# Attention weights times values as three rounded products, and row sums turned through DRAM, in a hybrid mLSTM and attention encoder layer

## The chip, the cores and the metric

The kernel runs on one core of a Trainium2 chip. The metric is the device time of one execution in microseconds. Where three runs are shown, the median is given with the lowest and the highest. A profile is one execution taken by the hardware profiler; its span is the time between its first and last instruction.

The engines are named as in the profile: PE is TensorE (matmuls; PEld are its weight loads), DVE is VectorE, ACT is ScalarE, POOL is GpSimd, and SP is SyncE, which here only starts transfers. SPq, ACTq and POOLq are the instruction queues that start a DMA.

## The reference

One layer of an encoder is applied to 2048 prompt tokens and to 256 sample tokens with the same weights (D = 1024), and a final RMSNorm follows:

```
h = rmsnorm(x); p = h @ w_in
x = x + concat(mlstm(p), attention(p)) @ w_out          # 8 mLSTM heads, 8 attention heads of 64
h = rmsnorm(x); u = dwconv3(h @ w_up)                   # 2 x 2816 channels
x = x + (silu(g) * a) @ w_down ;  y = rmsnorm(x)
```

The change is in the attention. It has 8 query heads and 2 key/value heads, is bidirectional, and q and k are RMS-normed and rotated:

```
s = einsum('bqhgd,bkhd->bhgqk', q, k) * 64 ** -0.5      # per block of queries
p = softmax(s, axis=-1)
o = einsum('bhgqk,bkhd->bqhgd', p, v)
```

All inputs and outputs are float32. The prompt's 2048 queries see 2048 keys, the sample's 256 queries see 256 keys.

## The kernel before, in words

The 2304 tokens are 18 tiles of 128. A matmul of two float32 tiles is one product in the code and two matmul records in the profile. The large products are written as three *rounded* products instead (dtype float32r): an operand x is kept as hi = round(x) and lo = x - hi, and hi·hi + hi·lo + lo·hi are accumulated.

**Phase A** (`phase_a`, the first 230 us or so) takes one token tile after the other: `front_a` loads x and computes its mean square, `front_b` normalises it and splits it into hi and lo, `mm` multiplies it with the attention and gate columns of w_in, and `post_a`, `post_b`, `post2` make q, k and v and store them to DRAM (`q_d`, `k_d`, `v_d`). `gates` prepares the mLSTM gates. `gate_math` follows.

**Attention and mLSTM** run side by side (`run_both` takes steps of both generators in a fixed ratio). A planner with a timeline simulation then sets the order on each engine, by priorities and by when it takes an instruction to be ready. Each engine works through its own order. Parts of mLSTM have a raised priority (`MPRI`), and once the output projection runs, so has the attention (`APRI`).

The attention works in 36 blocks of 512 columns: 32 large ones (one head, 512 prompt queries, 16 key tiles) and 4 small ones (two heads, the 256 sample queries, 2 key tiles), so 32 x 16 + 4 x 2 = 520 key tiles in all. The small blocks of the first head group come first, those of the second come last. For each block:

- `prep` transposes q. `maxstep` multiplies queries with keys (tile px) and DVE takes the row maximum (L546, L547); the next block's 16 max steps are done during the present block. `prep2` turns the negated maxima into an extra row of the query operand.
- `scores` takes key tiles in pairs (a step, kp): two rounded products (L569, L570) put scores minus maximum into a PSUM tile ps, and ACT writes the exp to a float32 tile pe in SBUF (L571).
- `values`, two pairs later (`PLAG` = 2), multiplies pe with the value tile vv (L581), which holds 64 columns of v and 64 columns of ones; so rows 64 to 127 of the result pv are 64 copies of the softmax sum.
- `fin1` copies both halves of pv to SBUF (o1, rs: L589, L590). `fin2` takes the reciprocal of the 64x512 sums on DVE (L594), multiplies on POOL (L595) and stores to `mix_d` (L598).

The PSUM tiles with the tag "sc" (ps, px, the transposed q, and the maxima) share a ring of `SCB` = 4 banks, given out in the order of the program; pv has one bank. mLSTM has one bank for projections and two for the rest. `load_kv` loads keys and values of a head group over POOL's queue.

**Phase C** (`phase_c`) is the output projection. It begins when mLSTM is done and takes 256 tokens at a time, as soon as their attention output is complete: it loads `mix_d` (L934), splits it (L935, L936) and multiplies (L949), then adds x, squares and norms (L954, L957, L966). It still runs when the attention is finished. **Phase D** (from about 1900 us on) is the feed-forward part with the final norm; the change doesn't touch it.

Two lines of the kernel on which the attention's timing hangs, the ring and the lag:

```
ps = pp.tile([P, 512], F32, tag="sc", ...)      # ring of SCB = 4 PSUM banks, shared with px, pq, pr
if kp >= PLAG: values(cur, *todo.pop(0))        # PLAG = 2 pairs behind the scores
```

## Time and profile before

| | before |
|---|---|
| median of 3 runs | 3498.3 us (3497.74 to 3503.58) |
| the profiled execution's own time | 3496.09 us |
| its span | 3494.4 us |
| mean granted TensorE clock | 0.991 |
| PE busy | 3401.6 us, 97% |
| DVE busy | 2346.9 us, 67% |
| ACT busy | 1680.2 us, 48% |
| POOL busy | 1101.4 us, 32% |
| HBM read, written | 315.55 MB, 82.72 MB |

Busy times are sums over an engine's instructions without those that only start transfers, and overlapping instructions are counted once. Matmuls are pipelined: a matmul's own duration is longer than the time after which the next one starts, and the ends are modelled. The "granted clock" is the share of full speed that TensorE was given. In a list of groups a line reads: source line, engine, operation, output<-inputs, shapes and count, then the busy time and the mean duration in ns of one, then the idle time of the engine just before them and what ended it. In a list of waits: who waited, for whom, us in total, how many times, the longest.

### The profile page before, as it was taken

What the parts mean: (1) busy time and instruction counts of PE and PEld (TensorE: products, weight loads), DVE (VectorE), ACT (ScalarE), POOL (GpSimd) and SP (SyncE); (2) the same over time, 40 slices, a digit from 0 to 9 for tenths busy, and PEclk for the clock granted to TensorE, in tenths of its full rate; (3) what the DMA queues carried; (4) which work ended last, traced back from release to release, by engine and by line L of the source; (5) the groups of instructions that cost most, each with busy time, mean ns of one, the idle gap of its engine ahead of it and who ended that gap; (6) DMA issues with size and microseconds to landing.
All of it is one profiled execution on the core that took longest, in us unless ns stands there. A gap on an engine that the chain in (4) does not pass through costs nothing. (4 is left out here: it accounts for less than half of the span.)

```text
span 3494.4 us, 53250 instructions
## 1 busy us (share of the span) xinstructions
PE 3401.6 (97%) x19538; PEld 3027.3 (87%) x19538; DVE 2346.9 (67%) x4008; ACT 1680.2 (48%) x3809; POOL 1101.4 (32%) x1298
## 2 busy tenths in 40 slices
PE   7999999999999999999999999999999999999998
PEld 6788777777777777767788999998999999999998
DVE  6874364546544555664445888878888878887777
ACT  4544354444444454453333544445544445555555
POOL 6752022213231321311125333225433224422222
PEclk9999999999999999999999999999999999999999
DMA  6764233233243434442247332213423213312221
GB/s 218 244 196 135 81 119 96 83 119 95 89 128 111 136 112 136 130 138 79 86 157 249 120 105 96 73 69 122 143 98 103 73 67 124 140 63 70 73 68 54
DMA packets 252629, 401.76 MB, mean 115 GB/s; under 512 B 27984, under 2 KB 152688, under 8 KB 252368
## 3 DMA queue, kind: packets, MB, share of 16 engines
q1 hardware_dynamic: 220272, 355.87, 30.5%
q0 software_dynamic: 10640, 31.86, 3.1%
q10 hardware_dynamic: 21456, 10.62, 1.0%
q8 instruction: 154, 2.52, 0.3%
q14 instruction: 107, 0.88, 0.1%
HBM read 315.55 MB, written 82.72 MB: 114 GB/s over the span
## 5 line engine op out<-in xcount | busy, mean ns | idle before, releaser
L1203 PE MATMUL pd<-act,wd 128*128 128x384 f32 (+1 forms) x3120 | 591.2, 335 | 17.0 <-DVE acc L1205 11.3
L1203 PEld LDWEIGHTS pd<-act,wd 128*128 128x128 f32 x3120 | 539.5, 188 | 24.0 <-DVE acc L1205 14.7
L581 PE MATMUL pv<-pe,vv 128*128 128x512 f32 x1040 | 514.5, 593 | 0.2
L547 DVE TENSOR_REDUCE mx<-px 128x1 f32<-128x512 f32 (+1 forms) x528 | 342.5, 673 | 194.2 <-PE px L546 192.5
L1065 PE MATMUL pa<-nt,wut 128*128 128x386 f32 (+2 forms) x2376 | 455.0, 339 | 1.5 <-ACT u L1081 1.5
L1065 PEld LDWEIGHTS pa<-nt,wut 128*128 128x128 f32 x2376 | 422.2, 190 | 1.8 <-ACT u L1081 1.8
L571 ACT ACTIVATE pe<-ps 128x512 f32<-128x512 f32 x520 | 292.5, 595 | 262.2 <-PE ps L570 258.6
L1159 DVE SCALAR_TENSOR_TENSOR y<-u,cw,y 128x768 f32<-128x768 f32 (+1 forms) x264 | 307.9, 1167 | 36.0 <-ACT y L1152 29.0
L1070 POOL TENSOR_TENSOR tw<-ru 128x512 f32<-128x512 f32 x66 | 96.4, 1461 | 744.5 <-DMA ru<-w_up 536.5
L1205 DVE TENSOR_TENSOR acc<-pd,acc 128x384 f32<-128x384 f32 (+1 forms) x544 | 281.4, 538 | 37.5 <-PE pd L1203 36.5
L1081 ACT ACTIVATE u<-pa 128x386 f32<-128x386 f32 (+2 forms) x264 | 128.8, 488 | 327.1 <-PE pa L1065 325.0
L581 PEld LDWEIGHTS pv<-pe,vv 128*128 128x128 f32 x1040 | 189.0, 189 | 82.5 <-issue 57.8
L569 PE MATMUL ps<-qq,kk 128*128 128x512 f32 x520 | 249.8, 483 | 0.1
L949 PE MATMUL po<-cmx,wo 128*128 128x256 f32 x1728 | 241.7, 290 | 1.6 <-DVE wo L106 1.6
L949 PEld LDWEIGHTS po<-cmx,wo 128*128 128x128 f32 x1728 | 220.8, 190 | 25.4 <-issue 17.8
L546 PE MATMUL px<-kk,qq 128*128 128x512 f32 (+1 forms) x528 | 224.4, 455 | 2.6 <-ACT pe L571 1.7
L688 PE MATMUL mj<-mn,wm 128*128 128x256 f32 x1296 | 212.2, 303 | 5.8 <-ACT og L702 4.5
L688 PEld LDWEIGHTS mj<-mn,wm 128*128 128x128 f32 x1296 | 180.7, 193 | 34.7 <-issue 20.6
L570 PE MATMUL ps<-qm,kl 65*128 65x512 f32 x520 | 207.4, 402 | 0.0
L698 PE MATMUL mv<-wm,mn 128*128 128x256 f32 x1296 | 206.3, 298 | 0.9 <-ACT qb L694 0.9
L698 PEld LDWEIGHTS mv<-wm,mn 128*128 128x128 f32 x1296 | 178.4, 192 | 22.3 <-issue 14.2
L232 PE MATMUL pj<-w_a,n1T 128*128 128x512 f32 (+1 forms) x864 | 178.9, 362 | 5.7 <-ACT n1T L188 4.5
(283 smaller groups left out, 6629.8 us busy)
## 6 DMA issues: line engine op xcount, KB each, us to landing
ru<-w_up SPq DMA_DIRECT2D x132, 512.0 KB, 3.2
mn<-n_d SPq DMA_DIRECT2D x216, 256.0 KB, 3.3
rd<-w_down SPq DMA_DIRECT2D x66, 512.0 KB, 3.3
n_d<-n1T SPq DMA_DIRECT2D x18, 1024.0 KB, 5.6
dm<-nm_d POOLq DMA_DIRECT2D x72, 256.0 KB, 3.6
mjn<-n_d SPq DMA_DIRECT2D x72, 256.0 KB, 3.0
mvn<-n_d SPq DMA_DIRECT2D x72, 256.0 KB, 3.2
q_d<-qz SPq DMA_DIRECT2D x18, 512.0 KB, 3.1
```

The costliest lines, as they stand in the source:

```text
L546: nc.tensor.matmul(ps[:, 0:w], s.qq[:, t * P:(t + 1) * P], s.kv[z0][0][:, 0:w], start=True, stop=True)
L547: nc.vector.tensor_reduce(s.mx[:, t, z0:z0 + 1], ps[:, 0:w], AX.X, ALU.max)
L569: nc.tensor.matmul(ps[:, 0:N], kk[:, kc:kc + P], s.qq[:, 0:N], start=True, stop=False)
L571: nc.scalar.activation(pe[:, z, 0:N], ps[:, 0:N], AF.Exp)
L581: nc.tensor.matmul(s.pv[:, 0:N], s.kv[kp // 2][2][:, kt % 4, :], pe[:, z, 0:N], start=(kt == 0), stop=(kt == s.nk - 1))
L688: nc.tensor.matmul(pj[:, o], s.w[c][:, a, o * P:(o + 1) * P], nT[c][:, :, h, :], start=(c + o + k == 0), stop=(c == NCC - 1 and k == 2 and ...
L698: nc.tensor.matmul(pv[:, o], nT[c][:, o, a, :], s.w[c][:, h, 256:512], start=(c + o + k == 0), stop=(c == NCC - 1 and k == 2 and o == 1))
L949: nc.tensor.matmul(po[:, o], wo[c][z // 2][:, a, n], mx[c][:, h, :], start=(c == 0 and k == 0), stop=(c == NCC - 1 and k == 2))
L1065: nc.tensor.matmul(p, w[:, aa, c, :], ops[k][:, c, bb, 0:n], start=c == 0 and i == 0 and not add, stop=c == NCC // 2 - 1 and i == 2, skip_ ...
L1159: nc.vector.scalar_tensor_tensor(y[:, s:e], u[:, s + k:e + k], cw[:, k, jj:jj + 1], y[:, s:e], ALU.mult, ALU.add)
L1203: nc.tensor.matmul(po, wds[j][c // 4][:, aa, c % 4 * P:(c % 4 + 1) * P], acts[j][:, bb, z0:z1], start=(j == 0 and k == 0), stop=(j == len( ...
L1205: nc.vector.tensor_tensor(accs[c][:, z0:z1], po, accs[c][:, z0:z1], ALU.add)
```

## The change

What it does:

- **Values.** The exp is written back into its PSUM tile. ACT then copies it, rounded, to a tile ph in SBUF (`PHB` = 6 buffers), and DVE subtracts ph from the PSUM tile to a rounded tile pl (`PLB` = 6). v is stored as hi and lo in phase A (one more subtract on DVE; two stores over SP's queue instead of one over ACT's), loaded as two tiles, with ones in the hi tile's and zeros in the lo tile's extra columns. `values` makes three rounded products, vh·ph, vl·ph and vh·pl, of each float32 one.
- **Sums.** `fin1` copies one row of sums, and ACT's queue stores it to DRAM (`rs_d`). SP's queue loads it back as 128x4. `fin2` (at step 1 of the next block) takes the reciprocal of the 128x4 tile on DVE, stores it and loads it broadcast to 64 rows, both over SP's queue. `fin3` (at step 4, or at the block's last step) multiplies on POOL and stores to `mix_d`.
- **Phase A.** x is loaded by `load_x`, one tile earlier, over SP's queue for the first four tiles and over POOL's from then on. Of the gates' copies the one to gp goes from DVE to POOL and the one to rows from DVE to ACT.
- In mLSTM's `out_a` the load of the output gate is ordered behind the load of dm on POOL's queue.

```diff
--- before.py
+++ after.py
@@ -68,7 +68,8 @@
 RW = 4
 PO = 4
 PB = 4
-PEB = 5
+PHB = 6
+PLB = 6
 PLAG = 2
 ZT = 3
 SG = 3
@@ -164,11 +165,15 @@
 
         xs = {}
 
+        def load_x(i):
+            n = order.index(i)
+            xs[i] = x = xw[n] if n < NX0 else sx.tile([P, NCC, P], F32, tag="x", name=f"x{i}", bufs=3)
+            (nc.sync if n < 4 else nc.gpsimd).dma_start(x, g.xT[i])
+
         def front_a(i):
 
             n = order.index(i)
-            x = xw[n] if n < NX0 else sx.tile([P, NCC, P], F32, tag="x", name=f"x{i}", bufs=3)
-            nc.sync.dma_start(x, g.xT[i])
+            x = xs[i]
             xq = sx.tile([P, NCC, P], F32, tag="xq", name=f"xq{i}", bufs=2)
             nc.scalar.activation(xq, x, AF.Square, scale=1.0 / 32.0)
@@ -239,9 +244,12 @@
 
             qk = sp.tile([P, 10, HD], F32, tag="qk", name=f"qk{i}")
             nc.scalar.activation(qk, pj[:, 0:640].rearrange("p (h d) -> p h d", d=HD), AF.Copy)
-            v = sp.tile([P, 2, HD], F32, tag="v", name=f"v{i}", bufs=2)
-            nc.scalar.activation(v, pj[:, 640:768].rearrange("p (h d) -> p h d", d=HD), AF.Copy)
-            nc.scalar.dma_start(g.v_d[:, :, i, :].rearrange("g p d -> p g d"), v)
+            v = sp.tile([P, 2, 2, HD], F32R, tag="v", name=f"v{i}", bufs=2)
+            pv = pj[:, 640:768].rearrange("p (h d) -> p h d", d=HD)
+            nc.scalar.activation(v[:, 0], pv, AF.Copy)
+            nc.vector.tensor_tensor(v[:, 1], pv, f32(v[:, 0]), ALU.subtract)
+            for a in range(2):
+                g.st.dma_start(g.v_d[a, :, :, i].rearrange("g p d -> p g d"), f32(v[:, a]))
             gt = g.gtm[:, i]
             nc.vector.tensor_tensor(gt, pj[:, 768:800].rearrange("p (a k) -> p a k", a=2),
                                     bgb.rearrange("p (a k) -> p a k", a=2), ALU.add)
@@ -296,12 +304,12 @@
                 if i % 2 == 0:
                     yield
                 gp = gps[i % 3]
-                nc.vector.tensor_copy(gp.rearrange("p a (b z) -> p a b z", b=2)[:, :, :, 0:8],
+                nc.gpsimd.tensor_copy(gp.rearrange("p a (b z) -> p a b z", b=2)[:, :, :, 0:8],
                                       g.gtm[:, i].rearrange("p a (b h) -> p a b h", b=2))
                 pg = pp.tile([40, 2, P], F32, tag="pk", name=f"pg{i}")
                 for a in range(2):
                     nc.tensor.transpose(pg[:, a, :], gp[:, a, 0:40], g.ident)
-                nc.vector.tensor_copy(g.rows[:, :, i * P:(i + 1) * P], pg)
+                nc.scalar.activation(g.rows[:, :, i * P:(i + 1) * P], pg, AF.Copy)
 
         def post2(i, kz):
             pk = pp.tile([P, 2, P], F32R, tag="pk", name=f"pk{i}")
@@ -311,17 +319,22 @@
             nc.scalar.activation(kT, f32(pk), AF.Copy)
             nc.scalar.dma_start(g.k_d[:, :, i * P:(i + 1) * P].rearrange("g p t -> p g t"), f32(kT))
 
+        load_x(order[0])
         front_a(order[0])
...
+        load_x(order[4])
         front_a(order[3])
@@ -347,6 +360,8 @@
                     tables2(slice(2 * n + 2, min(2 * n + 4, NT1)))
                 if wm:
                     wm.pop(0)()
+            if n + 5 < NT:
+                load_x(order[n + 5])
             if n + 4 < NT:
                 front_a(order[n + 4])
             if n == NT - 1:
@@ -479,18 +494,20 @@
             s = f"{n}_{t0}"
             kk = sp.tile([P, m * P], F32R, tag="kk" + s, name=f"kk{grp}_{s}", bufs=1)
             kl1 = sp.tile([65, m * P], F32R, tag="kl1" + s, name=f"kl1{grp}_{s}", bufs=1)
-            vv = sp.tile([P, m, P], F32, tag="vv" + s, name=f"vv{grp}_{s}", bufs=1)
+            vs = [sp.tile([P, m, P], F32R, tag=f"v{a}" + s, name=f"v{a}{grp}_{s}", bufs=1) for a in range(2)]
             c = slice((k0 + t0) * P, (k0 + t0 + m) * P)
             if after is not None:
-                for t in (kk[0:1, 0:1], kk[HD:HD + 1, 0:1], kl1[0:1, 0:1], vv[0:1, 0, 0:1]):
+                for t in (kk[0:1, 0:1], kk[HD:HD + 1, 0:1], kl1[0:1, 0:1], vs[0][0:1, 0, 0:1], vs[1][0:1, 0, 0:1]):
                     nc.gpsimd.tensor_copy(t, after[0:1, 0:1])
-            nc.gpsimd.memset(vv[:, :, HD:P], 1.0)
+            for a in range(2):
+                nc.gpsimd.memset(f32(vs[a][:, :, HD:P]), 1.0 - a)
             for r in (0, HD):
                 nc.gpsimd.dma_start(f32(kk[r:r + HD, :]), g.k_d[grp, 0:HD, c])
             nc.gpsimd.dma_start(f32(kl1[0:HD, :]), g.k_d[grp, HD:P, c])
             nc.gpsimd.memset(f32(kl1[64:65, :]), 1.0)
-            nc.gpsimd.dma_start(vv[:, :, 0:HD], g.v_d[grp, :, k0 + t0:k0 + t0 + m])
-            parts.append((kk, kl1, vv))
+            for a in range(2):
+                nc.gpsimd.dma_start(f32(vs[a][:, :, 0:HD]), g.v_d[a, grp, :, k0 + t0:k0 + t0 + m])
+            parts.append((kk, kl1, vs))
 
     class HB:
         pass
@@ -561,45 +578,63 @@
 
     def scores(s, kp):
         N = s.N
-        pe = sp.tile([P, 2, 512], F32, tag="pe", name=f"pe{s.nm}_{kp}", bufs=PEB)
+        parts = []
         for z in range(2):
-            ps = pp.tile([P, 512], F32, tag="sc", name=f"ps{s.nm}_{kp}_{z}")
+            ps = pp.tile([P, 512], F32, tag="sc", name=f"ps{s.nm}_{kp}_{z}")[:, 0:N]
             kk, kl1, _ = s.kv[kp // 2]
             kc = (2 * kp + z) % 4 * P
-            nc.tensor.matmul(ps[:, 0:N], kk[:, kc:kc + P], s.qq[:, 0:N], start=True, stop=False)
-            nc.tensor.matmul(ps[:, 0:N], kl1[:, kc:kc + P], s.qm[:, 0:N], start=False, stop=True)
-            nc.scalar.activation(pe[:, z, 0:N], ps[:, 0:N], AF.Exp)
-        return kp, pe
-
-    def values(s, kp, pe):
+            nc.tensor.matmul(ps, kk[:, kc:kc + P], s.qq[:, 0:N], start=True, stop=False)
+            nc.tensor.matmul(ps, kl1[:, kc:kc + P], s.qm[:, 0:N], start=False, stop=True)
+            ph, pl = (sp.tile([P, 512], F32R, tag=t, name=f"{t}{s.nm}_{kp}_{z}", bufs=n)[:, 0:N]
+                      for t, n in (("ph", PHB), ("pl", PLB)))
+            nc.scalar.activation(ps, ps, AF.Exp)
+            nc.scalar.activation(ph, ps, AF.Copy)
+            nc.vector.tensor_tensor(pl, ps, f32(ph), ALU.subtract)
+            parts.append((ph, pl))
+        return kp, parts
+
+    def values(s, kp, parts):
 
         N = s.N
         if kp == 0:
             s.pv = pp.tile([P, 512], F32, tag="pv", name="pv" + s.nm, bufs=1)
-        for z in range(2):
+        for z, (ph, pl) in enumerate(parts):
             kt = 2 * kp + z
-            nc.tensor.matmul(s.pv[:, 0:N], s.kv[kp // 2][2][:, kt % 4, :], pe[:, z, 0:N], start=(kt == 0),
-                             stop=(kt == s.nk - 1))
+            vh, vl = (v[:, kt % 4, :] for v in s.kv[kp // 2][2])
+            for k, (v, p) in enumerate(((vh, ph), (vl, ph), (vh, pl))):
+                nc.tensor.matmul(s.pv[:, 0:N], v, p, start=(kt == 0 and k == 0), stop=(kt == s.nk - 1 and k == 2))
 
     def fin1(s):
 
         N = s.N
         s.o1 = sp.tile([HD, 512], F32, tag="o1", name="o1" + s.nm, bufs=2)
-        s.rs = sp.tile([HD, 512], F32, tag="rs", name="rs" + s.nm, bufs=1)
+        s.rs = sp.tile([1, 512], F32, tag="rs", name="rs" + s.nm, bufs=1)
+        nc.scalar.activation(s.rs[:, 0:N], s.pv[HD:HD + 1, 0:N], AF.Copy)
         nc.scalar.activation(s.o1[:, 0:N], s.pv[0:HD, 0:N], AF.Copy)
-        nc.scalar.activation(s.rs[:, 0:N], s.pv[HD:P, 0:N], AF.Copy)
+        s.n = len(done)
+        done.append(s)
+        nc.scalar.dma_start(g.rs_d[s.n:s.n + 1, 0], s.rs)
+        s.rc = sp.tile([P, 4], F32, tag="rc", name="rc" + s.nm, bufs=2)
+        nc.sync.dma_start(s.rc, g.rs_d[s.n, 0].rearrange("(p k) -> p k", k=4))
 
     def fin2(s):
+
+        nc.vector.reciprocal(s.rc, s.rc)
+        nc.sync.dma_start(g.rs_d[s.n, 1].rearrange("(p k) -> p k", k=4), s.rc)
+        s.rb = sp.tile([HD, 512], F32, tag="rb", name="rb" + s.nm, bufs=1)
+        nc.sync.dma_start(s.rb, g.rs_d[s.n:s.n + 1, 1].to_broadcast([HD, 512]))
+
+    def fin3(s):
         N = s.N
-        nc.vector.reciprocal(s.rs[:, 0:N], s.rs[:, 0:N])
-        nc.gpsimd.tensor_tensor(s.o1[:, 0:N], s.o1[:, 0:N], s.rs[:, 0:N], ALU.mult)
+        nc.gpsimd.tensor_tensor(s.o1[:, 0:N], s.o1[:, 0:N], s.rb[:, 0:N], ALU.mult)
         for t0, (h, q0, q1) in part(s):
             r0 = HD * (h % 2)
             nc.gpsimd.dma_start(g.mix_d[q0 // 2:q1 // 2, r0:r0 + HD, 4 + h // 2].rearrange("n p t -> p n t"),
-                           s.o1[:, t0 * P:(t0 + q1 - q0) * P].rearrange("p (n t) -> p n t", t=BT))
+                                s.o1[:, t0 * P:(t0 + q1 - q0) * P].rearrange("p (n t) -> p n t", t=BT))
             if h == 7:
                 g.mixed.update(range(q0, q1))
 
+    done = []
     cur = prep(0)
     while cur.todo:
         maxstep(cur)
@@ -625,9 +660,12 @@
                     maxstep(nxt)
                 if not nxt.todo:
                     prep2(nxt)
-            if old is not None and (nxt is None or not nxt.todo or kp == nkp - 1):
-                fin2(old)
-                old = None
+            if old is not None:
+                if kp == min(1, nkp - 1):
+                    fin2(old)
+                if kp == min(4, nkp - 1):
+                    fin3(old)
+                    old = None
             yield 2.2
         for t in todo:
             values(cur, *t)
@@ -639,6 +677,7 @@
             prep2(nxt)
         old, cur = cur, nxt
     fin2(old)
+    fin3(old)
 
 
 def mlstm(g, tc, s1, sp, sw, sn, pj_, pm):
@@ -782,7 +821,7 @@
         nm = f"{s.p}_{i}"
         o = Pair()
         o.dm = sp.tile([P, 2, 2, P], F32, tag="dm", name="dm" + nm, bufs=DMB)
-        nc.gpsimd.dma_start(o.dm.rearrange("p d h l -> p (d h l)"),
+        ins = nc.gpsimd.dma_start(o.dm.rearrange("p d h l -> p (d h l)"),
                           g.nm_d[i, 4 * s.p:4 * s.p + 4].rearrange("r l -> (r l)").unsqueeze(0).to_broadcast([P, 4 * P]))
         for d in range(2):
             sgn = 1 - 2 * d
@@ -794,7 +833,8 @@
         if s.p < LASTP:
             if i % 2 == 0:
                 s.og = s1.tile([P, 2, P], F32, tag="ogT", name="ogr" + nm, bufs=OTB)
-                nc.gpsimd.dma_start(s.og, g.og_d[s.p, i // 2])
+                with tc.issue_after(ins.ins):
+                    nc.gpsimd.dma_start(s.og, g.og_d[s.p, i // 2])
             o.og = s.og[:, i % 2]
         return o
 
@@ -1292,7 +1332,8 @@
         dram("x1_d", [NB, P, NCC, BT])
         dram("q_d", [NT, P, 8, P])
         dram("k_d", [2, P, T])
-        dram("v_d", [2, P, NT, HD])
+        dram("v_d", [2, 2, P, NT, HD])
+        dram("rs_d", [36, 2, 512])
         dram("nm_d", [NT, 16, P])
         dram("og_d", [4, NB, P, 2, P])
         g.ident = kp.tile([P, P], F32, name="ident")
```

3 lines of the change are left out of this document (added).

## The prediction

> **What bounds the kernel now.** I read the page's totals first, then the busy times by stretch, the groups of instructions, the order of TensorE's instructions in time, and last the waits. The totals and the slices say that TensorE has work almost all the time, at full clock, and that nobody else is near that.
>
> ```profile
> PE 3401.6 (97%) x19538; PEld 3027.3 (87%) x19538; DVE 2346.9 (67%) x4008; ACT 1680.2 (48%) x3809; POOL 1101.4 (32%) x1298
> PE   7999999999999999999999999999999999999998
> PEclk9999999999999999999999999999999999999999
> ```
>
> The change works in the first half, so the view by stretches decides. Columns: length, then busy us (instructions) of PE, PEld, DVE, ACT, POOL, then clock, DMA share, GB/s.
>
> ```profile
> 0.00:300.00 300.00, 264.21 (x1573) 231.63 (x1574) 219.99 (x418) 140.00 (x240) 181.24 (x251) 0.97 0.67 220
> 300.00:1100.00 800.00, 796.45 (x4447) 622.79 (x4446) 389.05 (x833) 369.97 (x1044) 182.71 (x364) 1.00 0.31 99
> 1100.00:1500.00 400.00, 394.31 (x2184) 305.27 (x2182) 230.92 (x582) 193.57 (x584) 110.25 (x227) 1.00 0.41 130
> 1500.00:1800.00 300.00, 296.98 (x1640) 228.26 (x1639) 150.94 (x276) 122.77 (x252) 45.95 (x50) 1.00 0.32 99
> 1800.00:1900.00 100.00, 97.92 (x817) 97.41 (x815) 45.60 (x83) 26.36 (x50) 43.50 (x43) 1.00 0.79 254
> 1900.00:3494.00 1594.00, 1551.68 (x8888) 1541.96 (x8888) 1310.43 (x1820) 827.47 (x1641) 537.70 (x364) 0.99 0.27 94
> ```
>
> From 300 to 1800 us (attention beside mLSTM, then beside the output projection) TensorE is busy for 796.45 + 394.31 + 296.98 = 1487.7 of 1500 us. Only 12.3 us are idle, so a microsecond of TensorE work saved there is a microsecond of time, as long as nobody makes it wait. ACT is busy for 369.97 + 193.57 + 122.77 = 686 us (46%), DVE for 771 us (51%). After the attention, 1800 to 1900 us is the output projection alone, again at 98%: an earlier end of the attention is passed on.
>
> The groups that the change touches, then DVE's copies of the gates (with 18 instructions each):
>
> ```profile
> L581 PE MATMUL pv<-pe,vv 128*128 128x512 f32 x1040 | 514.5, 593 | 0.2
> L547 DVE TENSOR_REDUCE mx<-px 128x1 f32<-128x512 f32 x512 | 336.6, 681 | 186.2 <-PE px L546 184.6
> L571 ACT ACTIVATE pe<-ps 128x512 f32<-128x512 f32 x520 | 292.5, 595 | 262.2 <-PE ps L570 258.6
> L594 DVE RECIPROCAL rs<-rs 64x512 f32<-64x512 f32 x36 | 120.2, 3340 | 87.7 <-ACT rs L590 87.6
> L954 DVE TENSOR_TENSOR cx<-po,cx 128x512 f32<-128x512 f32 x36 | 24.7, 685 | 72.9 <-PE po L949 72.9
> L304 DVE COPY rows<-pg 40x256 f32<-40x256 f32 x18 | 7.2, 406 | 0.2 <-PE pg L303 0.2
> L299 DVE COPY gp<-gtm 128x32 f32<-128x32 f32 x18 | 3.9, 244 | 0.1
> ```
>
> The mean of a matmul (593 ns) is no price, since matmuls overlap. Prices come from starts in the order of time (start us, us, engine, line):
>
> ```profile
> 641.85 0.39 PE L570 MATMUL ps<-qm,kl 65*128 65x512 f32 x1
> 642.08 0.40 PE L569 MATMUL ps<-qq,kk 128*128 128x512 f32 x1
> 642.32 0.40 PE L570 MATMUL ps<-qm,kl 65*128 65x512 f32 x1
> ...
> 643.01 0.39 PE L767 MATMUL mu<-va,kw 128*128 128x130 f32 x2
> ...
> 647.62 1.02 PE L581 MATMUL pv<-pe,vv 128*128 128x512 f32 x2
> 648.08 0.79 PE L569 MATMUL ps<-qq,kk 128*128 128x512 f32 x1
> 648.71 0.40 PE L570 MATMUL ps<-qm,kl 65*128 65x512 f32 x1
> ```
>
> Five rounded (float32r) 512-column matmuls start between 641.85 and 643.01 (two lines are left out), 0.232 us each. A float32 product of values is two records: 647.62 to 648.71 is 1.09 us and holds that product and one rounded matmul (648.08), so the product takes 1.09 - 0.232 = 0.858 us.
>
> **The change part by part.**
>
> *Values.* L581 has 1040 / 2 = 520 products. Each becomes three rounded ones: 3 x 0.232 = 0.696 us, a saving of 0.162 us, or 84 us in all. The neighbouring gaps are 0.23 to 0.24 us, which bounds it at 87 and 72 us. The new operands have the form of L569 (128 rows, 512 columns), so I take 84. The Trainium skill ("FP8 and Floating Point Precision", TensorE Precision Notes) says that true FP32 is four passes through the array; three passes for four would save 0.858 / 4 = 0.215 us, an estimate of 112 us and a sum of 3401. The rows here make a rounded product 0.232 and not 0.215 us, and I go by them.
>
> *ACT.* Per key tile one 128x512 copy is added, out of PSUM. L571 is the same traffic, 595 ns alone and 292.5 / 520 = 563 ns in a row: 520 x 0.595 = +309 us. The exp now writes PSUM, which no row shows. The nearest row is L571 itself (0.595); as bounds I take 0.3 (a faster write) and twice the row, 1.19 us. At 0.595 ACT comes to 686 + 309 = 995 us of a stage of about 1416, 70%; at 1.19 it would be 92% and all but the bound.
>
> *DVE.* Per key tile one subtract with a PSUM and an SBUF operand is added, the form of L954: 520 x 0.685 = +356 us. The reciprocal over 64x512 goes (36 x 3.34 = 120 us) and one over 128x4 comes, of the form of L829:
>
> ```profile
> 651.55 0.18 DVE L829 RECIPROCAL dn<-dn 128x4 f32<-128x4 f32 x1
> ```
>
> That is 36 x 0.18 = 6 us. DVE in the stage: 771 + 356 - 120 + 6 = 1013 us, 72%.
>
> Neither engine becomes the bound by its sum, so their cost is what they make TensorE wait. Two rows of the stretches bracket it: with DVE at 49% (300 to 1100) TensorE idles 3.55 of 800 us, 0.4%; with DVE at 82% (1900 on) 42.3 of 1594, 2.7%. At 72% a straight line gives 2.0% of 1416 = 28 us, against 12.3 before: +16 us, with 0 and +26 as ends.
>
> *Sums through DRAM.* These transfers stand in for the new ones (16-byte pieces and a broadcast of one row have no row of their own):
>
> ```profile
> mix_d<-mmx ACTq DMA_DIRECT2D x54, 64.0 KB, 2.2
> mix_d<-mmx SPq DMA_DIRECT2D x18, 64.0 KB, 1.8
> bq<-q_d SPq DMA_DIRECT2D x32, 256.0 KB, 2.7
> ```
>
> Store 2.2, load 2.7, reciprocal 0.18, store 1.8, load 2.7: 9.6 us in a row. The work is spread over the next block's steps (the reciprocal at step 1, the multiplication at step 4, a step being about 5.8 us), and POOL and DVE find their operands there. Before, POOL sat waiting for the reciprocal; what is late next there is the last load. The loads also hold up SP, which stands behind each store until it has landed: 36 x (2.2 + 1.8) = 144 us of SP's time. Behind it are mLSTM's loads of activations, which mostly wait for TensorE to free their buffers:
>
> ```profile
> SPq L685 <- PE mv L698: 510.8, 165, 25.6
> PE mj L688 <- DMA mn<-n_d: 1.3, 1, 1.3
> POOL o L595 <- DVE rs L594: 152.7, 26, 23.6
> ```
>
> Ends: 0, and 14 us if one in ten of these stops reaches TensorE. I take +4, since of 216 such loads one was late. The exception is the end. The last large block's chain is here (POOL multiplies, stores; ACT casts the loads for the next block of the projection; TensorE goes on with the current one):
>
> ```profile
> 1781.93 0.60 ACT L590 ACTIVATE rs<-pv 64x512 f32<-64x512 f32 x1
> 1788.17 1.28 POOL L595 TENSOR_TENSOR o<-o,rs 64x512 f32<-64x512 f32 x1 [5.81 <-DVE m4r L555]
> 1797.29 0.42 ACT L935 ACTIVATE cmx<-cmx 128x256 fp32r<-128x256 f32 x1 [1.74 <-DMA cmx<-mix_d]
> 1800.87 0.62 ACT L957 ACTIVATE csq<-cx 128x512 f32<-128x512 f32 x1
> ```
>
> From the sums (1782.53) to POOL took 5.6 us; it becomes 9.6 or more, 4 us later. The first cast at 1797.29 comes some 3 us before the current block's last square (1800.87). So little cover is left: +3, ends 0 and +6.
>
> *x loads and copies.* The loads go to POOL's queue, one tile earlier. TensorE's waits at the front:
>
> ```profile
> ACT xq L173 <- DMA x<-xT: 21.7, 7, 6.3
> PE rs_a L127 <- POOL sq L180: 8.0, 4, 3.3
> PE pj L232 <- ACT n1T L188: 4.5, 3, 2.9
> ```
>
> At best 8.0 + 4.5 = 12.5 us go. DVE is relieved of 7.2 + 3.9 us of copies and gets 18 small subtracts in their place (at most 0.4 us each by L304, 7 us). The v stores go from ACT's queue to SP's, ahead of the n1 and q stores there; only loads that run tiles ahead stand behind them. POOL pays for 14 loads. I take -6, between 0 and -12. The larger buffers of v and of the weights, the extra fills and loads by POOL (twice as many for v) and the order of the og load I cost at nothing: they lie under TensorE's 99% in the stage, and would show as POOL waits if that cover went.
>
> Sum, against the profiled execution's 3496.1 us (span 3494.4; the median of the three runs, 3498.3, is 2 us above): 3496.1 - 84 + 16 + 4 + 3 - 6 = 3429 us. Its ends: 3496 - 87 - 12 = 3397, and 3496 - 72 + 26 + 14 + 6 = 3470.
>
> **The rivals.**
>
> *A. Everything is hidden.* No new waits and the whole front gain: 3397 us. For it: DVE at 82% still leaves TensorE 97%. Against: the chain from score to value now crosses ACT twice and DVE once.
>
> *B. The PSUM ring sets the pace: slower.* Four banks serve two scores and on average two max steps per pair of key tiles, so a bank comes round once per pair, 1500 / 260 = 5.77 us before and 5.45 after. A bank is now free only after exp, copy and subtract. From a pair's first matmul the second bank's path is 0.46 + 4 x 0.6 (ACT takes both tiles) + 0.685 = 3.55 us, and it is wanted at 5.45 + 0.46: 2.36 us of slack. The other work per pair is (686 - 292) / 260 = 1.5 us on ACT, (771 - 337 - 120) / 260 = 1.2 on DVE, and two max steps of 0.68: 4.1 us together, in queues kept in order. If more than 2.36 us of it stands ahead, TensorE waits for the rest, in order too; the gain of 67 us is used up at 2.36 + 67 / 260 = 2.62 us. At two thirds (2.8 us) it is 0.44 x 260 = +114, so 3543 us. For it: before, a bank was free after one ACT operation, and still the scores waited for it a little:
>
> ```profile
> PEld ps L569 <- ACT pe L571: 5.8, 19, 0.9
> ```
>
> Against: those 5.8 us are small, and mLSTM or projection matmuls stand between the steps. The Trainium skill ("ScalarE: Activation LUTs", step by step, the note on ScE to PSUM) calls PSUM the faster target for ScalarE, with the caveat that it helps only if TensorE doesn't need most of PSUM. No row here shows such a write; of PSUM's banks four are this ring, one holds pv and three are mLSTM's.
>
> *C. Part of B.* Waits of 40 to 65 us in place of 16: 3453 to 3478 and a little beyond, about 3475.
>
> *D. It doesn't do what it says.* If the rounded products came at 0.286 us or more in this place, 84 us would be nothing: 3513. Against: no rounded 512-column row stands that far apart.
>
> **How the numbers follow.** A tenth to A (0.10), 0.58 to the sum (its own range 3400 to 3465), 0.15 to C, 0.12 to B, 0.03 to D, 0.02 to no change. Faster by over 0.2% (7 us, about what a measurement here can tell): 0.83; slower 0.15; same 0.02. Range 3397 to 3500: above lie B and D, below little.
>
> **What would show it.** PE rows of the values: 1560 records, the next start 0.23 us on. The stage would be some 60 to 70 us shorter, with ACT near 70% and DVE near 72%. Waits of scores or max steps for the new DVE subtract above 40 us in all speak for C, above 100 for B. ACT's wait for x should go. ACT above 85% in the stage would mean that the exp into PSUM is dear. Wrong it would be if TensorE's idle time in the stage passes 80 us, or if a load of activations is what TensorE waits for.

## The result, and the profile after

The changed kernel takes 3531.15 us (median of four runs, 3528.60 to 3539.88) against 3498.97 us for the kernel before in the same call (3497.74 to 3503.58). The ratio is 1.0096, with a 95% interval of 1.0084 to 1.0109: slower by about 34 us, where 67 us less was predicted. The profiled execution took 3530.07 us, with a span of 3528.3 us.

The totals and the slices of the changed kernel, then its busy times by stretch (columns as before):

```profile
PE 3364.8 (95%) x20058; PEld 3133.6 (89%) x20058; DVE 2560.3 (73%) x4510; ACT 1953.6 (55%) x4347; POOL 1115.3 (32%) x1354
PE   7999999999999999899988999999999999999998
```

```profile
300.00:1100.00 800.00, 775.39 (x4886) 691.19 (x4885) 502.83 (x1147) 504.09 (x1346) 202.87 (x411) 0.98 0.39 114
1100.00:1500.00 400.00, 373.39 (x2233) 320.54 (x2233) 281.96 (x691) 261.73 (x704) 102.79 (x201) 0.98 0.45 133
1500.00:1800.00 300.00, 286.06 (x1761) 249.85 (x1760) 190.88 (x352) 159.35 (x306) 43.13 (x42) 0.99 0.30 89
1800.00:1900.00 100.00, 88.36 (x533) 74.75 (x533) 42.36 (x82) 49.24 (x93) 23.52 (x25) 0.92 0.40 121
```

In the slices, of 88 us each, TensorE falls to eight tenths at the 17th (1411 to 1499 us) and at the 21st and 22nd (1764 to 1941 us), where it had nine before. It works 37 us less over the whole span, and yet the span is 34 us longer. From 300 to 1800 us it idles 1500 - 775.39 - 373.39 - 286.06 = 65.2 us, where it was 12.3. The granted clock, 1.00 before, is 0.98 on average from 300 to 1900 us: by the trace's record of the clock TensorE ran at half of it for 61 us of that stretch, against 7 before, and at half clock rounded products start 0.43 us apart instead of 0.23 (rows in the last section). That costs an estimated 27 us, half of the difference. No other engine is near its limit: from 300 to 1500 us ACT is busy for 64% and DVE for 65%. The feed-forward part took about as long as before (1598 us against 1594): its first rounded matmul starts 30 us later, at 1930.2 us instead of 1900.6, and that is nearly the whole loss.

The new operations came at the prices that the prediction took (columns: busy us, mean ns, idle before):

```profile
L592 DVE TENSOR_TENSOR pl<-ps,ph 128x512 fp32r<-128x512 f32 x520 | 352.7, 686 | 248.7 <-ACT ph L591 240.5
L590 ACT ACTIVATE ps<-ps 128x512 f32<-128x512 f32 x520 | 298.0, 586 | 191.9 <-PE ps L587 187.7
L591 ACT ACTIVATE ph<-ps 128x512 fp32r<-128x512 f32 x520 | 302.5, 598 | 8.1
```

And rounded products of values follow each other at 0.23 us, in order of time:

```profile
639.74 0.40 PE L605 MATMUL pv<-pl,v 128*128 128x512 f32 x1
639.98 0.62 PE L605 MATMUL pv<-ph,v 128*128 128x512 f32 x2
640.44 0.39 PE L605 MATMUL pv<-pl,v 128*128 128x512 f32 x1
```

So the loss is not in a price. It is in when things happen. The next view lists the value products after mLSTM's last mN matmul, of the changed kernel and then of the kernel before (first and last start at the end of each row). One pl product stands for one key tile in the first, two records for one in the second:

```profile
L605 PE MATMUL pv<-pl,v x156: 388/395/796, 1439.2 to 1847.6; 128*128 128x512 f32 x156
```

```profile
L581 PE MATMUL pv<-pe,vv x192: 590/592/676, 1527.3 to 1798.9; 128*128 128x512 f32 x192
```

mLSTM was done 88 us earlier, at 1437.3 instead of 1525.7 us, but the attention was behind: 156 key tiles were left, against 96. They took 408 us instead of 272, with little but the output projection beside them, and the attention ended 49 us later. So mLSTM had gone ahead, and the attention had fallen behind.

TensorE's idle time lies on both sides of mLSTM's end. Up to there and from there to the end of the attention, in the changed kernel:

```profile
300.00:1437.00 1137.00, 1093.73 (x6813) 965.24 (x6811) 741.43 (x1755) 722.56 (x1961) 299.28 (x604) 0.98 0.41 119
1437.00:1848.00 411.00, 384.28 (x2239) 326.14 (x2238) 259.45 (x483) 239.06 (x464) 51.82 (x53) 0.98 0.31 91
```

And in the kernel before:

```profile
300.00:1526.00 1226.00, 1216.77 (x6746) 945.88 (x6745) 637.21 (x1457) 577.47 (x1663) 298.16 (x600) 1.00 0.34 108
1526.00:1799.00 273.00, 269.98 (x1517) 209.69 (x1515) 132.70 (x232) 108.43 (x215) 40.74 (x41) 1.00 0.33 103
```

TensorE idles 43.3 us before mLSTM's end, where it was 9.2, and 26.7 us after it, where it was 3.0. So the larger part is lost while mLSTM still runs.

What held the attention up shows in one place of the changed kernel, in order of time over all engines:

```profile
658.10 0.40 PE L586 MATMUL ps<-qq,kk 128*128 128x512 f32 x1
...
658.77 0.58 ACT L590 ACTIVATE ps<-ps 128x512 f32<-128x512 f32 x1 [5.19 <-PE ps L587]
...
659.05 0.39 PE L586 MATMUL ps<-qq,kk 128*128 128x512 f32 x1
...
662.88 1.28 ACT L831 ACTIVATE dm<-dm,tm 128x128 f32<-128x128 f32 x4 [3.53 <-POOL dm L828]
663.16 0.66 POOL L732 MEMSET qb<- 64x256 f32 x2
664.07 0.57 ACT L591 ACTIVATE ph<-ps 128x512 fp32r<-128x512 f32 x1
664.54 0.58 ACT L590 ACTIVATE ps<-ps 128x512 f32<-128x512 f32 x1
664.67 0.69 DVE L592 TENSOR_TENSOR pl<-ps,ph 128x512 fp32r<-128x512 f32 x1 [2.98 <-ACT ph L591]
664.69 0.30 PEld L605 LDWEIGHTS pv<-ph,v 128*128 128x128 f32 x2 [1.80 <-ACT ph L591]
664.69 0.73 PE L605 MATMUL pv<-ph,v 128*128 128x512 f32 x2 [1.60 <-ACT ph L591]
```

The scores go into a bank at 658.10, the exp is over at 659.35, but the copy stands in ACT's order behind mLSTM's exp (L831), which waits 3.53 us for POOL. The subtract ends at 665.36. The bank was held for 7.3 us, 6.0 of them after the exp. Pairing the 520 rows of L586 with the 520 of L592 in order of time, from the start of the first to the end of the second, a bank is held for 4.42 us on average. For the kernel before (L569 to the end of L571) it is 1.94 us.

### The profile page after: what moved, and what is told of

It is laid out like the page before. It is cut to its first block, busy times and chain, and to the rows that moved or that the text cites. A ratio compares the mean times of both kernels' runs of the same rounds, so it can differ in the third digit from the quotient of the medians.

```text
span 3528.3 us, 56125 instructions
## 1 busy us (share of the span) xinstructions
PE 3364.8 (95%) x20058; PEld 3133.6 (89%) x20058; DVE 2560.3 (73%) x4510; ACT 1953.6 (55%) x4347; POOL 1115.3 (32%) x1354
## 5 line engine op out<-in xcount | busy, mean ns | idle before, releaser
L592 DVE TENSOR_TENSOR pl<-ps,ph 128x512 fp32r<-128x512 f32 x520 | 352.7, 686 | 248.7 <-ACT ph L591 240.5
L590 ACT ACTIVATE ps<-ps 128x512 f32<-128x512 f32 x520 | 298.0, 586 | 191.9 <-PE ps L587 187.7
L605 PE MATMUL pv<-ph,v 128*128 128x512 f32 x1040 | 343.9, 407 | 27.7 <-ACT ph L591 25.5
L591 ACT ACTIVATE ph<-ps 128x512 fp32r<-128x512 f32 x520 | 302.5, 598 | 8.1
L989 PEld LDWEIGHTS po<-cmx,wo 128*128 128x128 f32 x1728 | 233.1, 193 | 27.6 <-ACT cmx L975 12.2
L605 PEld LDWEIGHTS pv<-ph,v 128*128 128x128 f32 x1040 | 180.8, 191 | 66.0 <-ACT ph L591 37.5
L586 PE MATMUL ps<-qq,kk 128*128 128x512 f32 x520 | 216.8, 420 | 3.9 <-DVE mx L564 1.9
L563 PE MATMUL px<-kk,qq 128*128 128x512 f32 (+1 forms) x528 | 209.1, 415 | 7.5 <-DVE mx L564 3.9
L605 PE MATMUL pv<-pl,v 128*128 128x512 f32 x520 | 211.2, 406 | 3.3 <-DVE pl L592 3.2
L727 PE MATMUL mj<-mn,wm 128*128 128x256 f32 x1296 | 201.3, 292 | 9.7 <-ACT og L741 8.2
```

What stands on the lines that cost most here:

```text
L586: nc.tensor.matmul(ps, kk[:, kc:kc + P], s.qq[:, 0:N], start=True, stop=False)
L590: nc.scalar.activation(ps, ps, AF.Exp)
L591: nc.scalar.activation(ph, ps, AF.Copy)
L592: nc.vector.tensor_tensor(pl, ps, f32(ph), ALU.subtract)
L605: nc.tensor.matmul(s.pv[:, 0:N], v, p, start=(kt == 0 and k == 0), stop=(kt == s.nk - 1 and k == 2))
L727: nc.tensor.matmul(pj[:, o], s.w[c][:, a, o * P:(o + 1) * P], nT[c][:, :, h, :], start=(c + o + k == 0), stop=(c == NCC - 1 and k == 2 and ...
```

## The experiments

The theory that came out of this, **the ring**: the four PSUM banks that scores and max steps share are held too long, and attention falls behind because of that. Rivals: **the load** (more passes on ACT and DVE, whatever holds the bank), **the order** (ACT's second pass behind mLSTM's exp, whatever holds the bank), **the balance** (the factor by which the planner lets mLSTM run ahead), **the sums** and **the front**. A ratio is always to the kernel before in the same call, with its 95% interval.

### Parts of the change alone

Only the new values:

> The values part alone (three rounded products, exp in PSUM, copy and subtract); sums and front as before. If the copies on ACT and DVE and the wait for them eat the gain (ACT or ring theory): 3515 to 3540 us, TensorE idle in the attention as in the full change. If the sums through DRAM eat it (POOL sat 241 us waiting for them): 3430 to 3455 us.

Measured: 3519.27 us, ratio 1.0059 (1.0037 to 1.0080), the number of the ACT or ring theory. Slower by itself: the part that was to save 84 us costs 21. mLSTM ended at 1363 us, with some 180 key tiles left.

Only the sums through DRAM:

> The sums through DRAM alone, values as one float32 product, front as before. ACT or ring theory: within 10 us of before, 3490 to 3505. Sums theory: 3530 us or more, since the same waits of POOL and SP are there. The 114 us that DVE is spared should gain little, as DVE is not the bound.

Measured: 3535.52 us, ratio 1.0096 (1.0079 to 1.0112): 34 us, where +7 was predicted, and the number of the theory of the sums. Here mLSTM ended later than before, at 1563 us, with 92 key tiles left: that is not the picture of the whole change, so the sums seem to lose their time in another way.

Only the front part (x loads, small copies, order of the og load):

> The kernel before with only the front part (loads of x by POOL one tile earlier, the two small copies moved, the order of the og load). By the prediction's step: 3486 to 3498 us, ratio 0.9966 to 1.000. If the front part takes part in the loss: above 1.001.

Measured: 3502.95 us, ratio 1.0007 (0.9998 to 1.0016): nothing, and between the ranges of both theories. ACT's wait for x is here and in the whole change no smaller than the 21.7 us of before:

```profile
ACT xq L177 <- DMA x<-xT: 29.4, 9, 7.0
```

```profile
ACT xq L178 <- DMA x<-xT: 21.8, 6, 7.1
```

The parts do not add up (21 + 34 + 2 us alone, 34 together), so the losses overlap. Which of them overlap, these runs don't tell.

### One pass less

```diff
-            nc.vector.tensor_tensor(pl, ps, f32(ph), ALU.subtract)
-            parts.append((ph, pl))
+            parts.append((ph, ph))
```

> The full change without the subtract: the third product takes ph again, so the low part of the weights is left out. TensorE's work is the same, DVE is 353 us lighter and a PSUM bank is free after the copy, 0.7 us earlier. Ring or DVE theory: most of the lost 115 us comes back, 3430 to 3460. ACT theory (the second pass over ACT makes the weights late): little comes back, 3505 to 3530.

Measured: 3469.06 us, ratio 0.9908 (0.9893 to 0.9924). The other way round, with one ACT pass less (the subtract then takes the scores):

```diff
-            nc.scalar.activation(ps, ps, AF.Exp)
-            nc.scalar.activation(ph, ps, AF.Copy)
+            nc.scalar.activation(ph, ps, AF.Exp)
```

> The full change with one pass on ACT: exp goes straight to ph, the subtract takes the scores, so the low part of the weights is wrong. TensorE's and DVE's work is the same, ACT is about 300 us lighter, a score bank is free 0.6 us earlier. ACT theory: most of the lost 115 us comes back, 3430 to 3460. DVE theory: 3505 to 3530. If both this and the run without the subtract gain about half, it is the length of the chain and not one engine.

Measured: 3485.53 us, ratio 0.9964 (0.9952 to 0.9976). The subtract is worth 66 us in this place, the ACT pass 46, and both times lie between the two ranges given for them. Each gives back about half of the lost time, which by the second expectation speaks for the length of the chain and not for one engine. But each run takes away load and holding time together (mean hold 3.36 and 3.03 us), so they don't tell load from ring.

### The same passes, the bank free after the exp

Exp to SBUF, with the values part alone (and one buffer in place of two for the attention's output o1):

```diff
+            pe = sp.tile([P, 512], F32, tag="pe", name=f"pe{s.nm}_{kp}_{z}", bufs=2)[:, 0:N]
-            nc.scalar.activation(ps, ps, AF.Exp)
-            nc.scalar.activation(ph, ps, AF.Copy)
-            nc.vector.tensor_tensor(pl, ps, f32(ph), ALU.subtract)
+            nc.scalar.activation(pe, ps, AF.Exp)
+            nc.scalar.activation(ph, pe, AF.Copy)
+            nc.vector.tensor_tensor(pl, pe, f32(ph), ALU.subtract)
```

> The values part alone (3519.3 us in its run), with the exp written to SBUF in place of PSUM, so that the bank of scores is free after the exp and the copy and the subtract read the SBUF tile. Theory of the ring (four banks, each held for exp, copy and subtract, set the pace): the time drops to at most 3490 us. Theory of the load (the two passes of ScalarE and the one of VectorE, in order among mLSTM's work, are what attention waits for): 3510 to 3525 us, the same as with the exp in PSUM.

Measured: 3448.83 us (3447.94 to 3453.08), ratio 0.9856 (0.9842 to 0.9871). The ring's number is beaten. The same edit in the whole change:

> The whole change (ratio 1.0096) with one edit: the exp goes to an SBUF tile, and ScalarE's copy and VectorE's subtract read that tile, so a bank of scores is free after the exp. ScalarE and VectorE have the same number of passes (buffers of the low part 5 in place of 6, of attention's output 1 in place of 2). Theory of the ring: what this edit gained with the values part alone (from 1.0059 to 0.9856, 70 us) comes here too: 3455 to 3475 us. Theory of the load and the order: at most 15 us of it, 3515 us or more.

Measured: 3475.50 us, ratio 0.9932 (0.9917 to 0.9947): 57 us less than with the exp in PSUM (1.0096 - 0.9932 = 0.0164 of 3499). The time is at the upper end of the ring's range. The theory of the load falls, because no pass got cheaper. The groups of the first of the two:

```profile
L582 DVE TENSOR_TENSOR pl<-pe,ph 128x512 fp32r<-128x512 f32 x520 | 370.3, 722 | 199.4 <-ACT ph L581 194.0
L580 ACT ACTIVATE pe<-ps 128x512 f32<-128x512 f32 x520 | 302.3, 592 | 148.6 <-PE ps L576 115.2
L581 ACT ACTIVATE ph<-pe 128x512 fp32r<-128x512 f32 x520 | 318.9, 629 | 7.4
```

All three take longer than with PSUM (592 against 586 ns, 629 against 598, 722 against 686). What fell is the time for which a bank is held, to 3.04 us and 2.95 us. In the trace of the whole change with this edit, the release reads like this:

```profile
654.87 0.48 PE L586 MATMUL ps<-qq,kk 128*128 128x512 f32 x1
...
655.61 1.09 ACT L591 ACTIVATE pe<-ps 128x512 f32<-128x512 f32 x2 [3.99 <-PE ps L587]
...
656.59 1.15 ACT L592 ACTIVATE ph<-pe 128x512 fp32r<-128x512 f32 x2
...
658.34 1.28 DVE L593 TENSOR_TENSOR pl<-pe,ph 128x512 fp32r<-128x512 f32 x2
```

The copies and subtracts follow, up to 659.62, but both banks are free at 656.70.

The order alone does not explain the loss either. ACT's wait for POOL in front of mLSTM's exp, from 300 to 1900 us, is as long as in the whole change (which comes first here), and yet the time is 57 us less:

```profile
ACT dm L831 <- POOL dm L828: 128.4, 50, 7.3
```

```profile
ACT dm L832 <- POOL dm L829: 126.5, 58, 7.8
```

One more rival gets an answer by this edit only in part: the lag of two pairs (`PLAG`), which may be too short for a chain of three passes. The edit leaves the lag as it was and the passes no shorter, and yet TensorE's waits for ph fall from 25.5 to 3.0 us (from 300 to 1850 us) and the loss is gone. A longer lag was not run.

Fewer key tiles are left when mLSTM ends, and they take about as long each (2.65 us against 2.62). After the last mN:

```profile
L606 PE MATMUL pv<-pl,v x108: 387/393/507, 1484.1 to 1770.2; 128*128 128x512 f32 x108
```

The same without the sums part gives what the sums cost then, and what the front part adds to the values:

> The change without the sums part, with the exp in SBUF. If the sums part costs its 36 us beside the faster values too: 3425 to 3450 us, the lowest so far. If the sums part costs only beside the slow values: within 10 us of the whole change with the exp in SBUF. Against the values part alone with the exp in SBUF (0.9856) it gives what the front part is worth: 0 to 12 us lower by the prediction.

Measured: 3470.76 us, ratio 0.9912 (0.9897 to 0.9927). Once the bank is free, the sums make a difference of 0.9932 - 0.9912, some 7 us, in the place of 34; the two intervals overlap. But the front part, which alone was worth nothing, makes a difference of 20 us here (0.9912 against 0.9856), where up to 12 us less were predicted. Both differences are no larger than what a new order alone can cost (see below).

### A ring of three banks, no instruction changed

```diff
-SCB = 4
+SCB = 3
```

On the values part with the exp in SBUF:

> The values part alone with the exp in SBUF (ratio 0.9856), with a ring of three banks in place of four and nothing else changed. Theory of the ring (bank time is what attention runs out of): most of the 70 us comes back, 3495 to 3530 us, mLSTM ends earlier (by 1400 us) and more than 150 key tiles are left. Theory that the reads of PSUM or the new order made the loss: within 15 us of 3449.

Measured: 3532.65 us, ratio 1.0096 (1.0080 to 1.0111): 84 us more, so all of the gain is gone, and slightly more than the theory's range allowed. mLSTM ended at 1336 us, with about 200 key tiles left. On the kernel before:

> The kernel before with a ring of three banks in place of four and nothing else changed. Theory of the ring: the kernel before, whose banks are free after one pass, loses less than the changed one did by holding them longer, 5 to 40 us (3505 to 3540). If banks don't matter: 3495 to 3503 us.

Measured: 3560.19 us, ratio 1.0176 (1.0159 to 1.0193). That is 62 us more, above the range of the theory. In both kernels one bank less costs more than 60 us, so the number of banks limits the attention; and the kernel before, with banks free after one pass, already had no bank to spare, which I had not expected to this extent.

### The order and the balance

Loading dm one tile earlier, so that mLSTM's exp should wait less for POOL in front of the attention's passes (`DMB` = 4, one buffer less for o1, and the load moved out of `out_a`):

```diff
-                os_[i] = out_a(s, i)
+                if i == 0:
+                    os_[0] = load_dm(s, 0)
+                if i + 1 < NT:
+                    os_[i + 1] = load_dm(s, i + 1)
+                out_a(s, i, os_[i])
```

On the whole change:

> The whole change, with mLSTM's load of dm issued one tile earlier (four buffers in place of three, one buffer less for attention's output). Theory of the order (mLSTM's exp waits in ScalarE's order for POOL, which waits for this load, and attention's second pass waits behind it): ScalarE's wait for dm (128 us) falls by more than half and the time drops to 3490 to 3515 us. Theory of the balance: 3522 to 3535 us, since what is left when mLSTM ends stays as large, or grows.

Measured: 3519.25 us, ratio 1.0060 (1.0044 to 1.0075): 12 us less, between the ranges of both theories. ACT's wait for dm did not fall by more than half: it is 115.0 us, against 128.4. On the values part with the exp in SBUF:

> The values part alone with the exp in SBUF (ratio 0.9856), with mLSTM's load of dm one tile earlier (four buffers; five of the low part in place of six). If ScalarE's wait for POOL costs by itself: 8 to 15 us lower, 0.981 to 0.983. If it cost only by holding banks behind it: within 5 us of 0.9856, or a few us above, as any new order may give.

Measured: 3447.83 us, ratio 0.9852 (0.9835 to 0.9868), against 0.9856 without it: nothing. But here ACT's wait for dm even grew, from 72.9 to 82.1 us. In neither kernel did the edit take away the wait that it was made for, so neither run tests what ACT's standing behind mLSTM costs.

The lead of mLSTM in the whole change:

```diff
-LEAD = 1.3
+LEAD = 1.0
```

> The whole change, with the factor by which the planner lets mLSTM run ahead of attention cut from 1.3 to 1.0. Theory of the balance (the 156 key tiles that are left when mLSTM ends, against 96 before, run without other work for TensorE): fewer are left, at most 120, and the time drops to 3480 to 3510 us. Theory of the order (ScalarE's second pass stands behind mLSTM's exp wherever the two are mixed): 3525 us or more, with more idle time of TensorE while mLSTM runs.

Measured: 3537.81 us, ratio 1.0095 (1.0071 to 1.0119). 140 key tiles were left in the place of 156, where at most 120 were expected, and no time was saved: the number of the theory of the order. In the values part with the exp in SBUF:

> The values part alone with the exp in SBUF, with the factor by which the planner lets mLSTM run ahead cut from 1.3 to 1.0. Theory of the balance: fewer than 118 key tiles are left when mLSTM ends and the time falls by 5 to 20 us (3430 to 3445). If the factor doesn't set the order: 3445 to 3455 us.

> The same with the factor raised to 1.6. Theory of the balance: more than 118 key tiles are left and the time rises by 5 to 20 us (3455 to 3470). If the factor doesn't set the order: 3445 to 3455 us.

Measured: 3471.61 us, ratio 0.9919 (0.9904 to 0.9934), with 108 key tiles left, and 3487.37 us, ratio 0.9965 (0.9954 to 0.9976), with 155, against 0.9856 and 118 at 1.3. Both are slower, the one against the theory of the balance, the other by more than it said. So a smaller factor helps in neither kernel. And an edit of this one factor, which changes nothing but the planner's order, costs 22 and 38 us here, so differences of 20 us between two such kernels should not be read as the price of the edited part.

### The sums

Reciprocal and multiplication later (pairs 3 and 7 of the next block in place of 1 and 4), with the sums part alone:

> The sums part alone (3535.5 us in its run), with the reciprocal at pair 3 of the next step in place of 1, and POOL's multiply at pair 7 in place of 4. Theory that POOL and VectorE stand in their order before a value that is still under way through DRAM, with mLSTM's loads behind them: POOL's wait for the returned sums (290 us with the sums part alone) falls below 100 us and the time to 3495 to 3515 us. Theory that the cost is the late store of the result or SP's queue: 3530 us or more.

Measured: 3534.54 us, ratio 1.0099 (1.0084 to 1.0114), the number of the second theory. But POOL's wait for the returned sums stayed (279.5 us from 300 to 1900 us, against 284.3), so the first theory was not put to the test. With a multiplier that never has to be waited for:

> The sums part alone (3535.5 us, ratio 1.0096) with all its transfers, but POOL multiplies by a tile of ones that is there from the start, so its output lacks the division by the sums; POOL never waits for the returned sums. Theory that POOL's wait in its order, with mLSTM's loads behind it, is the cost: 3490 to 3505 us. Theory that the transfers in SP's queue or VectorE's wait for the sums are the cost: 3525 us or more.

Measured: 3515.83 us, ratio 1.0045 (1.0028 to 1.0062), 18 us less, and between the two ranges. The waits of POOL from 300 to 1800 us, with the sums part alone and then with this edit:

```profile
POOL o L606 <- DMA rb<-rs_d: 258.4, 30, 32.8
```

```profile
POOL o L606 <- ACT o L590: 208.2, 31, 28.4
```

POOL's multiplication stands just as early in its order, and now waits for the attention's output itself. I take it that the planner's order, not the program's, decides where POOL stands. Neither run took POOL's wait away. The 18 us that go with the returned value are no more than a new order can cost, so where the 34 us come from is open.

### The runs beside each other

Hold is the mean time from the first scores matmul to the end of the last reader of the bank, worked out from the 520 pairs of rows.

| kernel | banks | hold, us | key tiles left at mLSTM's end | ratio |
|---|---|---|---|---|
| before | 4 | 1.94 | 96 | 1 |
| whole change | 4 | 4.42 | 156 | 1.0096 |
| values alone | 4 | 4.39 | 180 | 1.0059 |
| whole change, no subtract | 4 | 3.36 | 112 | 0.9908 |
| whole change, one ACT pass | 4 | 3.03 | 100 | 0.9964 |
| whole change, exp in SBUF | 4 | 2.95 | 108 | 0.9932 |
| values alone, exp in SBUF | 4 | 3.04 | 118 | 0.9856 |
| the same, ring of three | 3 | 2.41 | 200 | 1.0096 |
| before, ring of three | 3 | 1.90 | 183 | 1.0176 |

Long holds in a ring of four, and short rings, go with more key tiles left at mLSTM's end, and at both ends of the table with more time. In between the order isn't kept: the whole change with the exp in SBUF has the shorter hold and fewer tiles left than the values alone with it, and takes 27 us more. The profile of the run with one ACT pass is that of its slowest execution (3497.95 us, median 3485.53).

## Why the prediction was wrong

- **Values, -84.** Right as a price (0.23 us a product), and the values part with the bank released gains 50 us of it. It is TensorE's work, and it was realised only where TensorE had something to do.
- **ACT and DVE, +16 (0 to +26).** This is the step that failed. The loads were right (590 ns a pass was foreseen, and neither engine was full), but the waits were read off a line from DVE's share of busy time, whose second point comes from the feed-forward part, where no scores wait for a bank. What counts is for how long a bank is held: 4.42 us instead of 1.94. TensorE's idle time rose by 53 us from 300 to 1800 us, where 16 were predicted. The edit that frees the bank after the exp is worth 57 us in the whole change and 70 with the values alone.
- **Rival B (ring, 3543, 0.12)** named the right resource; the result lies 12 us below it. That nearness is in part luck: two thirds of the 4.1 us are 2.73 and not 2.8, which would have given some 3525, and the way in which the time was lost is not the one that it described. Its working set the second bank's path, from the pair's first matmul, at 3.55 us without a queue. Measured is a mean hold of 4.42 us for each bank from its own first matmul. The sign that the prediction gave for it did not come: waits of scores and max steps for the new subtract above 100 us. They come to this, from 300 to 1850 us:

```profile
PEld pv L605 <- ACT ph L591: 37.5, 36, 4.4
PE pv L605 <- ACT ph L591: 25.5, 21, 4.0
...
PEld ps L586 <- DVE pl L592: 8.5, 19, 1.3
PEld px L563 <- DVE pl L592: 6.6, 10, 1.5
```

  Some 15 us wait for the bank, by these rows; the two longest waits are for ph, the rounded exp. My reading is that the planner sees in its own timeline that a bank is not free and puts other work there, so that the wait shows up as order: more of mLSTM early, fewer key tiles done, and later a stretch in which nothing fills TensorE's gaps. That the three-bank runs, which change no instruction, also leave more key tiles for the end supports this. It is argued from the order, no run was made with the order held fixed, and it speaks of the 26.7 us idle after mLSTM's end. Of the 43.3 us before it, 15.7 end with a wait of TensorE for ph and 4.2 with one for the bank. TensorE's idle time was the better sign: 76.8 us from 300 to 1900 us, near the 80 that the prediction named but not past it.

- **What followed an idle time.** The prediction counted idle time alone and had no term for the clock. After the 1.60 us that ended at 664.69, TensorE ran at half clock for 3.4 us:

```profile
655.00:662.60 7.60, 7.60 (x53) 6.97 (x52) 6.07 (x14) 0.58 (x1) 2.66 (x4) 1.00 0.32 71
664.60:666.20 1.60, 1.48 (x6) 0.82 (x6) 1.34 (x3) 1.60 (x8) 0.32 (x2) 0.99 0.00 0
666.20:669.60 3.40, 3.40 (x10) 2.71 (x11) 2.33 (x5) 2.12 (x7) 0.62 (x1) 0.50 0.01 2
```

  The third column from the end is the granted clock: 1.00, 0.99, 0.50. The Trainium skill ("TensorE: Matmul & The Clock Gate", A second HAM failure mode: psum-queue depth-cycling) says that short idle times of TensorE in a cycle through PSUM's banks can make the clock go down and up again. These rows agree as far as they go; the prediction did not weigh it. The clock costs an estimated 27 us from 300 to 1900 us, as said above, and the idle time grew there by 63 us (76.8 against 14.3). Against the 84 us that the values were to save, that would be a loss of 6 us, and the feed-forward part started 30 us later; the rest isn't accounted for.
- **The exp into PSUM.** The prediction cited the Trainium skill ("ScalarE: Activation LUTs", step by step, the note on ScE to PSUM) for it. An exp into PSUM took 586 ns and one into SBUF 592, so the faster target is worth 6 ns. The Trainium skill's caveat, that TensorE must not need most of PSUM, fits what the runs with three banks show.
- **Sums, +4 and +3.** Alone they cost 34 us, five times the predicted sum. Beside the released bank the difference is some 7 us, which is the predicted number, but a new order alone can make more than that, so it confirms nothing. In the whole change as it is, their share can't be told from the ring's.
- **Front, -6 (0 to -12).** Wrong: alone +2 us with an interval that holds 0, and ACT's wait for x did not go.

The books from the prediction's -67 us to the measured +34: the bank 57; values with the released bank -50 instead of -84 + 16 = -68, so 18; the front part with the values 20 instead of -6, so 26; the sums 7, as predicted, so nothing. That is 101 us. Only the 57 is larger than what a new order alone can cost. The 26 is no price of the front part, since alone it costs nothing; why the order with it is 20 us worse is open. So the bank is shown as the cause of somewhat more than half of the miss.

The best version is the values part alone with the exp in SBUF: 3448.83 us, 1.4% below the kernel before. With the dm load earlier it is the same.

## What to carry to other kernels

Before a result stays in a PSUM bank for further passes, work out how long the bank is held from its first matmul to its last reader, with the queues that these readers stand in, and compare with the same kernel at one bank less: if that loses time, there is no slack to spend. A ring that is short need not show as waits for its banks where a planner fills the gaps with other work (here some 15 us of waits, and 57 us that its release gave back); look at how far each of the two streams has come at a fixed point, and at what is left for the end. A saving on the busiest engine is real only as long as there is work ready for it. Before reading a difference of two kernels as the price of an edit, run an edit that only makes the planner order anew, and see how much that alone changes.

## What the runs showed of the hardware

After an idle time of 1.60 us TensorE ran at half clock (0.50) for 3.4 us, and rounded matmuls then start 0.43 us apart instead of 0.23:

```profile
667.18 0.63 PE L586 MATMUL ps<-qq,kk 128*128 128x512 f32 x1
667.61 0.63 PE L587 MATMUL ps<-qm,kl 65*128 65x512 f32 x1
```

Not every such idle time did this. In the same kernel 2.30 us without a matmul, but for 0.04, were followed by full clock (1.00):

```profile
1699.10:1701.40 2.30, 0.04 (x1) 0.00 (x0) 0.43 (x1) 0.44 (x2) 0.00 (x0) 1.00 0.42 114
1701.40:1704.80 3.40, 3.37 (x23) 3.04 (x24) 2.90 (x7) 0.77 (x2) 0.00 (x0) 1.00 0.00 0
```

Of 128x512 passes, those that read the exp from SBUF were slower here than those that read it from PSUM: 629 against 598 ns for ACT's copy, and 722 (712 in the whole change with the exp in SBUF) against 686 ns for DVE's subtract, whose other operand lies in SBUF in both.
